# One step of a hybrid decoder on one core: rows before conditioning weights, output weights and samples first, one operation for the final norm

## The chip, the core and the metric

The kernel runs on one core of a Trainium2 chip. The metric is the device time of one execution in microseconds (us). TensorE (PE) multiplies, VectorE (DVE), ScalarE (ACT) and GpSimd (POOL) do the elementwise work, and the queue of SyncE (SP) issues nearly all loads and most stores. Every engine and every queue works through its own instructions in a fixed order that was laid down when the program was built.

## The reference, cut to what matters

One layer for a prompt of 2048 tokens and for 8 samples of 8 new tokens each (64 sample rows), all 1024 wide, in float32.

```python
ada = silu(c) @ w_ada + b_ada                  # conditioning: c is 1 + 8 rows, ada 6 x 1024 wide
sh_m, sc_m, g_m, sh_f, sc_f, g_f = split(ada, 6)
h = rmsnorm(x, norm_mix) * (1 + sc_m) + sh_m
rq, rk, rv, rg, sq, sk, sv = split(h @ w_in)
mix = concat(retention(rq, rk, rv) * silu(rg), stick_breaking(sq, sk, sv))
x = x + g_m * (mix @ w_out)
h = rmsnorm(x, norm_ffn) * (1 + sc_f) + sh_f
a = causal_conv3(h @ w_up_gate)
x = x + g_f * ((silu(a) * (h @ w_up_val)) @ w_down)
y = x * rsqrt(mean(x * x) + eps) * norm_final
```

The stick-breaking attention of the samples also reads 2048 cached positions per sample through a page table.

## The kernel before, in words

**Blocks and products.** The prompt is cut into four blocks of 512 tokens, each of four row tiles of 128 (`TILES`); the 64 sample rows ride with the first block in the projections and with the last block after attention. A float32 product is made of three products of a high and a low part (`mm3`, L310 to L312), or, for the 64 sample rows with their two parts side by side, of two (`tok_mm`, L319 and L320). A weight comes in as a 1 MB tile `raw` and is split into two tiles `whl`: ACT casts the high part (L183), DVE subtracts for the low part (L165).

**Who sets the order.** The functions are generators. `_weave` steps through several of them in proportion to the costs that they yield, and so fixes the order in which instructions are written down. A planner then runs through the instructions with a cost model of its own: on each engine and queue it takes, of those that are ready by its reckoning, the one written down first. So the order in the trace can differ from the order in the text, and on the chip each engine waits wherever the planned order puts something late in front.

**The head** (from L1490). The loads are written down in this order: conditioning rows `c9` and constants; the 2 MB of conditioning weights of column group 2 (a column group is 512 of the 6144 columns); the rows `hx` of the first block and of the samples (2.25 MB); column group 0; five small vectors into `vrows`; group 3 (into the two buffers of `wraw`); group 1. `ada` multiplies the conditioning rows by such a group (L531), copies the sums with ACT (L536), folds the partial sums by small products (L561) and writes coefficients with DVE (L568 or L572). It uses one buffer `ar`, into which the bias of each group is loaded in turn. `raw_features` norms each row tile (squares on ACT L399, root on POOL L392 and L165, scaling on DVE L590) and turns it on PE (L594, eight products a tile), with copies to `xT` (L598) that ACT and DVE share. `modulate` applies the coefficients of four of the eight feature groups k and splits the result into `act` (L605 to L612). Groups 2 and 0 serve k = 0 to 3, groups 3 and 1 serve k = 4 to 7. The first weights of the projection (`first_in`) are loaded and split after that, and `dense_pair` multiplies them: 96 products of 288 columns, 48 with k = 0 to 3 and 48 with k = 4 to 7. The caches' pages, the other conditioning groups and all four projection blocks follow, woven together, up to about 1240 us.

**The output block** (`out_block`). For the last block (`samp`) it loads, in this order, the gates of both halves (`load_g`), for each k the mixed features `act` and the samples' `smp` (eight loads of 64 KB), the rows `x` of the five tiles, and inside `w_tm` the output weights, two `raw` tiles for each half of 512 columns. Each k runs over the four row tiles and the samples; in the last two k of a half `by_tile` sorts by tile, the samples last. `residual` adds the result to `x`, `squares` and `rows_rstd` make the norm's root, and the generator `features` turns and modulates each tile for the next stage, the samples as the last of five. `ffn_block` of the block before drives it: one step before its last products (`next(feats, None)`), one after each of its four tiles, the rest after.

**The end** (`finish` inside `ffn_block`). The second half of each tile is squared by ACT (L1412), multiplied by the final weights `nf` by POOL (by DVE for the very last tile and in the other blocks), and, once POOL has made the root (`rows_rstd`), scaled by DVE with a one-tensor operation (L1417), beside ACT, which scales the first half (L1416). Then the tile is stored.

```python
            def finish(i, o, n, nf, eng):
                y = T(fp, [P, 2 * t], F32, "ff")
                act.activation(y[:n, :512], x2[i][:n, 512:], AF.Square, accum_out=ss[i][:n, 1:2])
                tt(eng, y[:n, 512:D], x2[i][:n, 512:], nf[:n], ALU.mult)
                yield
                r = rows_rstd(ss[i], n)
```

## Time and profile before

| what | us |
|---|---|
| median of 3 runs | 3336.03 (3325.15 to 3340.34) |
| the profiled execution, its own time | 3337.49 |
| its span, first to last instruction | 3335.8 |
| PE busy / DVE / ACT / POOL | 3201.6 / 2086.6 / 1580.0 / 1023.7 |
| mean granted TensorE clock | 0.98 of full |

A busy share says who works, not who is waited for; PE is busy for 96% of the span, so time can be won only where PE stands still, where it runs at the lower clock, or after its last product. The span is cut into stretches, and in each the instructions are read in order of time with the wait ahead of them. A row of such a list is: start, duration, engine, line, operation, result<-inputs, shapes and count, and in brackets the idle time of that engine just before and who ended it. Rows whose engine ends in q are a queue's issue of a transfer, not the transfer.

### The profile page before, as it was taken

The page shows a single profiled execution, that of the slowest core. Times are in us where ns is not written, and L with a number is a line of the kernel's source. Part 1 is how long each engine was busy: PE and PEld are TensorE (multiplying, and loading weights), DVE is VectorE, ACT ScalarE, POOL GpSimd, SP SyncE. Part 2 cuts the span into 40 slices and gives each one's busy share as a digit, 9 for nine tenths or more (in the row PEclk, how much of TensorE's full clock was granted, in tenths as well). Part 3 has the DMA queues.
Part 4 walks back from the last instruction along what each step waited for, and adds up shares of the span by engine and source line. Part 5 has one row for each costly group of instructions (what it writes and reads, how often), then busy time and mean ns, then how long its engine had stood idle before and what let it go on. Part 6 is the DMA issues. An engine that isn't in the chain of part 4 may idle for free. (4 is left out here: it accounts for less than half of the span.)

```text
span 3335.8 us, 50095 instructions
## 1 busy us (share of the span) xinstructions
PE 3201.6 (96%) x17879; PEld 2601.1 (78%) x17879; DVE 2086.6 (63%) x2989; ACT 1580.0 (47%) x2796; POOL 1023.7 (31%) x1841
## 2 busy tenths in 40 slices
PE   7999999999999889999999999999999999999998
PEld 5886777666887778878877778877788787799997
DVE  3245344245766587777778787787887873644445
ACT  3345335234444365555556455556555543533323
POOL 2012012013432343433444334344442432312113
PEclk8999999999999999999999999999999999999999
DMA  7757877885667843343454334354433335232221
GB/s 251 248 177 228 275 260 250 275 277 177 189 189 226 252 127 115 113 133 108 133 186 133 105 117 119 107 169 137 129 111 107 118 98 177 93 101 71 95 77 68
DMA packets 404247, 526.99 MB, mean 158 GB/s; under 512 B 25974, under 2 KB 242153, under 8 KB 403998
## 3 DMA queue, kind: packets, MB, share of 16 engines
q1 hardware_dynamic: 370078, 472.27, 45.3%
q10 hardware_dynamic: 33920, 51.52, 4.2%
q8 instruction: 142, 2.33, 0.3%
q14 instruction: 107, 0.88, 0.1%
HBM read 442.11 MB, written 81.60 MB: 157 GB/s over the span
## 5 line engine op out<-in xcount | busy, mean ns | idle before, releaser
L183 ACT CAST whl<-raw 128x1024 fp32r<-128x1024 f32 x408 | 427.5, 1049 | 1091.3 <-PE d L311 798.4
L165 DVE TENSOR_TENSOR whl<-raw,whl 128x1024 fp32r<-128x1024 f32 x408 | 517.8, 1270 | 577.0 <-ACT whl L183 568.8
L310 PE MATMUL d<-act,whl 128*128 128x512 f32 (+2 forms) x2016 | 745.0, 370 | 4.3 <-ACT whl L183 2.3
L312 PE MATMUL d<-act,whl 128*128 128x512 f32 (+2 forms) x2016 | 735.9, 365 | 1.2 <-DVE whl L165 1.2
L311 PE MATMUL d<-act,whl 128*128 128x512 f32 (+2 forms) x2016 | 733.7, 364 | 3.3 <-DVE act L165 2.4
L310 PEld LDWEIGHTS d<-act,whl 128*128 128x128 f32 x2016 | 384.8, 191 | 73.4 <-issue 11.1
L312 PEld LDWEIGHTS d<-act,whl 128*128 128x128 f32 x2016 | 383.9, 190 | 61.1 <-DVE whl L165 2.2
L311 PEld LDWEIGHTS d<-act,whl 128*128 128x128 f32 x2016 | 385.7, 191 | 58.7 <-DVE act L165 2.6
L310 PE MATMUL d<-whl,ff 128*128 128x512 f32 x704 | 279.3, 397 | 0.0
L311 PE MATMUL d<-whl,ff 128*128 128x512 f32 x704 | 278.8, 396 | 0.0
L312 PE MATMUL d<-whl,ff 128*128 128x512 f32 x704 | 278.1, 395 | 0.0
L310 PE MATMUL d<-whl,act 128*128 128x512 f32 x640 | 260.8, 409 | 10.3 <-ACT whl L183 9.2
L312 PE MATMUL d<-whl,act 128*128 128x512 f32 x640 | 258.5, 404 | 0.0
L311 PE MATMUL d<-whl,act 128*128 128x512 f32 x640 | 258.3, 404 | 0.0
L1172 DVE TENSOR_TENSOR_SCAN aom<-aom,acy 128x512 f32<-128x512 f32 x192 | 256.0, 1333 | 2.4 <-ACT aom L1158 1.7
L165 DVE TENSOR_TENSOR abe<-abe,aom 128x512 f32<-128x512 f32 (+2 forms) x320 | 229.7, 718 | 23.8 <-POOL abe L1162 2.3
L1196 PE MATMUL acc<-ahl,avv 128*128 128x512 f32 (+3 forms) x640 | 223.6, 410 | 15.2 <-DVE ahl L165 9.4
L1158 ACT ACTIVATE aom<-z,nb 128x512 f32<-128x512 f32 (+2 forms) x320 | 201.1, 628 | 61.2 <-PE z L1155 38.3
L1159 ACT ACTIVATE abe<-z,bb 128x512 f32<-128x512 f32 (+2 forms) x320 | 199.8, 624 | 0.0
L165 DVE TENSOR_TENSOR ahl<-z,ahl 128x512 fp32r<-128x512 f32 (+1 forms) x320 | 191.5, 598 | 10.7 <-ACT ahl L183 10.5
L1155 PE MATMUL z<-akk,aq 128*128 128x512 f32 (+3 forms) x640 | 190.5, 375 | 6.0 <-DVE ahl L165 3.1
L165 POOL TENSOR_TENSOR ff<-ff,hf 128x512 f32<-128x512 f32 (+1 forms) x101 | 161.0, 1624 | 90.2 <-DVE hf L165 76.2
(288 smaller groups left out, 5691.2 us busy)
## 6 DMA issues: line engine op xcount, KB each, us to landing
raw<-in_w_in SPq DMA_DIRECT2D x56, 1024.0 KB
raw<-in_w_up_gate SPq DMA_DIRECT2D x44, 1024.0 KB
raw<-in_w_up_val SPq DMA_DIRECT2D x44, 1024.0 KB
akk<-k SPq DMA_DIRECT2D x160, 256.0 KB
page<-in_cache_k_pages SPq DMA_DIRECT2D x128, 256.0 KB
vpage<-in_cache_v_pages SPq DMA_DIRECT2D x128, 256.0 KB
raw<-in_w_down SPq DMA_DIRECT2D x32, 1024.0 KB
raw<-in_w_ada SPq DMA_DIRECT2D x24, 1024.0 KB
```

The source lines that it names most:

```text
L165: eng.tensor_tensor(o, a, b, op)
L183: act.copy(hi, src)
L310: pe.matmul(ps, sh, mh, start=start, stop=False)
L311: pe.matmul(ps, sh, ml, start=False, stop=False)
L312: pe.matmul(ps, sl, mh, start=False, stop=stop)
L1155: pe.matmul(z[:, :n], qs[g, h][:, i * P : (i + 1) * P], kk[:, c, :n], start=c == 0, stop=c == 1)
L1158: act.activation(om[:, :n], z[:, :n], AF.Sigmoid, bias=nb[:, h : h + 1], scale=-SCALE)
L1159: act.activation(be[:, :n], z[:, :n], AF.Sigmoid, bias=bb[:, h : h + 1], scale=SCALE)
L1172: dve.tensor_tensor_scan(rv, rv, rv, init, ALU.mult, ALU.bypass)
L1196: pe.matmul(accs[0][:, cs], kv[u][1][:, kt, :], m[:, cs], start=(s == g and kt == 0 and c == 0), stop=(s == 0 and kt == NT - 1 and c == 1),)
```

## The change

The head: the four bias rows (into three `ar` buffers and one of the next pool) and the five vectors are loaded before the rows, the rows before any conditioning weights; groups 2 and 0 follow, then the first projection weights, then groups 3 and 1; the turns are written down ahead of all conditioning products, and the first half is modulated and the first weights are split ahead of groups 3 and 1. The output block of the last part: one load for all `smp`, the rows and gates written down after the second tile of output weights, the samples first in every loop, their features one step earlier. The end: `finish` loses its multiplication by `nf`, and the scaling after the root takes both factors in one operation (`scalar_tensor_tensor`), on DVE for all tiles.

```diff
@@ -209,7 +209,7 @@
...
     ]
-    mixs_sc = [T(dram, [P, 2, NS], F32, f"ms{k}") for k in range(KT)]
+    mixs_sc = T(dram, [KT, P, 2, NS], F32, "ms")
     gp_sc = [T(dram, [P, D], F32, f"gp{i}") for i in range(2)]
...
@@ -284,9 +284,13 @@
...
 
-    def w_fm(src, c0):
+    def raw_fm(src, c0):
         raw = next_raw().rearrange("p (a b) -> p a b", a=8)
         ld(raw, src[:, c0 : c0 + 256].rearrange("(k p) c -> p k c", p=P))
+        return raw
+
+    def w_fm(src, c0, raw=None):
+        raw = raw_fm(src, c0) if raw is None else raw
         for m in range(2):
...
@@ -361,7 +365,7 @@
...
         order = [(k, tile) for k in range(k0, k0 + 2) for tile in tiles]
-        return sorted(order, key=lambda kt: kt[1]) if k0 == n - 2 else order
+        return sorted(order, key=lambda kt: tiles.index(kt[1])) if k0 == n - 2 else order
 
...
@@ -491,7 +495,7 @@
...
     def vectors(pl):
-        rows = T(pl, [108, P], F32, "vrows")
+        rows = T(pl, [P, 512], F32, "hf")[:108, :P]
         for nme, o, n in (
...
@@ -518,15 +522,21 @@
...
 
+    def bias_row(pl, j):
+        ar = T(pl, [P, 512], F32, "ar")
+        ld(ar[P - 1 :, :], I["b_ada"][:, j * 512 : (j + 1) * 512])
+        return ar
+
     def ada(pl, s32, js, first=None):
...
         for j in js:
-            ar = T(pl, [P, 512], F32, "ar")
-            ld(ar[P - 1 :, :], I["b_ada"][:, j * 512 : (j + 1) * 512])
-            if first is not None:
+            if first is None:
+                ar = bias_row(pl, j)
+            else:
                 ps = pd()
-                for k0, raw in first.pop(j):
+                raws, ar = first.pop(j)
+                for k0, raw in raws:
                     for q in range(4):
...
@@ -534,7 +544,7 @@
...
                 act.copy(ar[: P - 1, :], ps[: P - 1, :])
-            else:
+            if first is None:
                 for k0, raw in w_rows(I["w_ada"][0], 0, KT, j * 512):
...
@@ -1252,12 +1262,13 @@
...
         xpool = xpools()
-        gates = [load_g(0, half, fp, samp and xpool) for half in range(2)]
+        ordered = tiles[NT:] + tiles[:NT]
         smp = T(xpool, [P, KT, 2, NS], F32R, "smp") if samp else None
+        gates = [] if samp else [load_g(0, half, fp, None) for half in range(2)]
         for k in range(KT):
             ld(acts[k // 4][:, k % 4, :, :TB], mix_sc[g][k])
-            if samp:
-                ld(smp[:, k], mixs_sc[k])
+        if samp:
+            ld(smp, mixs_sc.rearrange("k p c n -> p k c n"))
         x2, ss = [], []
...
@@ -1267,43 +1278,53 @@
...
 
-        for i, o, n in tiles:
-            x = T(xpool, [P, 1024], F32, "ff")
-            ld(x[:n], xp[g * TB + o : g * TB + o + n, :] if i < NT else xs)
-            x2.append(x)
-            ss.append(T(small, [P, 2], F32, f"os{i}"))
+        def rows():
+            if samp:
+                gates.append(load_g(0, 0, fp, xpool))
+            for i, o, n in tiles:
+                x = T(xpool, [P, 1024], F32, "ff")
+                ld(x[:n], xp[g * TB + o : g * TB + o + n, :] if i < NT else xs)
+                x2.append(x)
+                ss.append(T(small, [P, 2], F32, f"os{i}"))
+            if samp:
+                gates.append(load_g(0, 1, fp, xpool))
+
+        if not samp:
+            rows()
         for half in range(2):
...
             for k0, (hi, lo) in w_tm(w_out, 0, KT, half * 512):
-                for k, tile in by_tile(tiles, k0, KT):
+                if samp and half == 0 and k0 == 4:
+                    rows()
+                for k, tile in by_tile(ordered, k0, KT):
                     tok_mm(
...
                 tick()
-            for i, o, n in tiles:
+            for i, o, n in ordered:
                 residual(pss[i], gates[half][i == NT], x2[i], half, n, fp, dve if half else pool)
...
         tick(9)
-        rs = []
-        for i, o, n in tiles:
+        rs = {}
+        for i, o, n in ordered:
             squares(i, 1)
-            rs.append(rows_rstd(ss[i], n))
+            rs[i] = rows_rstd(ss[i], n)
 
...
                 if j >= 2:
-                    i, o, n = tiles[j - 2]
+                    i, o, n = ordered[j - 2]
                     to_features(xn[j - 2], o, n, coef[2], coef[3], acts, fp)
                 if j < len(tiles):
-                    i, o, n = tiles[j]
+                    i, o, n = ordered[j]
                     xa, xb = xn[j] = T(fp, [P, 512], F32, "c"), T(fp, [P, 512], F32, "a")
...
                     dve.tensor_scalar(xb[:n], x2[i][:n, 512:], rs[i][:n, 0:1], None, ALU.mult)
-                if j >= 1:
+                if j >= (2 if samp else 1):
                     yield 1.0
...
@@ -1407,14 +1428,13 @@
...
 
-            def finish(i, o, n, nf, eng):
+            def finish(i, o, n, nf):
                 y = T(fp, [P, 2 * t], F32, "ff")
                 act.activation(y[:n, :512], x2[i][:n, 512:], AF.Square, accum_out=ss[i][:n, 1:2])
-                tt(eng, y[:n, 512:D], x2[i][:n, 512:], nf[:n], ALU.mult)
                 yield
...
                 act.activation(y[:n, :512], x2[i][:n, :512], AF.Copy, scale=r[:n, 0:1])
-                dve.tensor_scalar(y[:n, 512:D], y[:n, 512:D], r[:n, 0:1], None, ALU.mult)
+                dve.scalar_tensor_tensor(y[:n, 512:D], x2[i][:n, 512:], r[:n, 0:1], nf[:n], ALU.mult, ALU.mult)
                 sv(O["y_prompt"][g * TB + o : g * TB + o + n, :] if i < NT else O["y_sample"], y[:n, :D])
...
@@ -1439,7 +1459,7 @@
...
                         residual(pss[tile[0]], gfs[half][tile[0] == NT], x2[tile[0]], half, tile[2], fp, dve)
-                        ends.append(finish(*tile, nf, pool if samp and tile[0] != NT - 1 else dve))
+                        ends.append(finish(*tile, nf))
                         next(ends[-1])
...
@@ -1490,28 +1510,24 @@
...
         with tile_pool("head", 2) as hp0:
-            hp = _Bufs(hp0, dict(hx=5, hj=1, xT=1, vrows=1, raw=4, ar=1))
-            rows_of = lambda j, pl=hp: list(w_rows(I["w_ada"][0], 0, KT, j * 512, pl))
-            xrows = first_rows(hp)
-            first = {2: rows_of(2)}
-            rows = list(xrows)
-            first[0] = rows_of(0)
+            hp = _Bufs(hp0, dict(hx=5, hj=1, xT=1, raw=4, ar=3))
+            rows_of = lambda j: list(w_rows(I["w_ada"][0], 0, KT, j * 512, hp))
+            bias = {j: bias_row(ip if j == 1 else hp, j) for j in (2, 0, 3, 1)}
             s32 = prep(hp, ip)
+            vectors(ip)
+            rows = list(first_rows(hp))
+            first = {j: (rows_of(j), bias[j]) for j in (2, 0)}
+            sq_raw = raw_fm(w_in, SQ)
             xT = T(hp, [P, KT, TB + NS], F32, "xT")
-            vectors(hp)
-            first[3] = rows_of(3, wraw)
-            feats = raw_features(hp, xT, rows)
-            for _ in ada(hp, s32, (2,), first):
+            for _ in raw_features(hp, xT, rows):
                 pass
-            for _ in feats:
+            for _ in ada(hp, s32, (2, 0), first):
                 pass
-            first[1] = rows_of(1)
-            for _ in ada(hp, s32, (0, 3), first):
+            first.update({j: (rows_of(j), bias[j]) for j in (3, 1)})
+            modulate(xT, coef[0], coef[1], acts, range(4))
+            first_in[0, 0, SQ] = list(w_fm(w_in, SQ, sq_raw))
+            for _ in ada(hp, s32, (3, 1), first):
                 pass
-            modulate(xT, coef[0], coef[1], acts, range(4))
-            for _ in ada(hp, s32, (1,), first):
-                pass
-            first_in[0, 0, SQ] = list(w_fm(w_in, SQ))
             modulate(xT, coef[0], coef[1], acts, range(4, 8))
...
```

## Rows read from the trace of the kernel before

**Rows 1.** Windows in the head: PE, PEld, DVE, ACT, POOL busy, clock, DMA share, GB/s.

```profile
20.00:30.00 10.00, 7.70 (x29) 1.13 (x21) 1.48 (x3) 0.00 (x0) 1.05 (x2) 1.00 1.05 382
...
50.00:60.00 10.00, 9.03 (x50) 8.64 (x49) 2.04 (x4) 3.94 (x6) 5.47 (x8) 0.50 0.20 72
...
90.00:100.00 10.00, 10.00 (x78) 9.98 (x77) 2.67 (x5) 2.88 (x7) 0.00 (x0) 1.00 1.03 322
```

**Rows 2.** PE in the head, in order of time.

```profile
27.79 1.92 PE L531 MATMUL d<-raw,s 128*32 128x512 f32 x2 [0.77 <-DMA raw<-in_w_ada]
...
31.37 6.94 PE L594 MATMUL z<-con,hx 128*128 128x128 f32 x36
...
46.46 0.61 PE L310 MATMUL d<-act,whl 128*128 128x288 f32 x1 [2.29 <-ACT whl L183]
...
71.00 0.29 PE L312 MATMUL z<-act,whl 128*128 128x288 f32 x1
```

**Rows 3.** DVE in the head: first rows scaled, and coefficients of both halves.

```profile
15.02 0.75 DVE L590 TENSOR_SCALAR hx<-hx,rs_b 128x1024 f32<-128x1024 f32 x1 [6.98 <-POOL rs_b L165]
...
41.71 0.20 DVE L568 COPY coef<-z 128x36 f32<-128x36 f32 x1 [2.94 <-PE z L561]
...
53.85 0.19 DVE L568 COPY coef<-z 128x36 f32<-128x36 f32 x1 [4.18 <-PE z L561]
```

**Rows 4.** SP's queue in the head.

```profile
2.96 1.96 SPq L171 DMA_DIRECT2D hx<-in_x_prompt  x4
...
9.95 2.21 SPq L171 DMA_DIRECT2D vrows<-in_norm_mix  x1
```

**Rows 5.** The last output block: DVE's split of the last down weights, SP's queue, the chain.

```profile
2804.77 1.23 DVE L165 TENSOR_TENSOR whl<-raw,whl 128x1024 fp32r<-128x1024 f32 x1 [3.76 <-ACT whl L183]
...
2814.96 1.50 SPq L171 DMA_DIRECT2D raw<-in_w_out  x2
...
2814.96 12.16 DMA raw<-in_w_out
```

**Rows 6.** PE in the last output block, and the window after its wait.

```profile
2828.30 1.22 PE L310 MATMUL d<-whl,act 128*128 128x512 f32 x2 [5.75 <-ACT whl L183]
...
2830.00:2840.00 10.00, 10.00 (x39) 7.93 (x39) 3.65 (x4) 1.99 (x2) 0.00 (x0) 0.86 0.30 107
```

**Rows 7.** Windows at the features of the last block, and its two releasing rows.

```profile
2880.00:2890.00 10.00, 6.61 (x38) 4.76 (x36) 7.45 (x14) 9.49 (x23) 3.93 (x3) 0.87 0.00 1
2890.00:2900.00 10.00, 7.30 (x36) 6.89 (x37) 8.99 (x26) 4.57 (x9) 3.04 (x4) 0.62 0.35 107
...
2889.94 0.68 DVE L165 TENSOR_TENSOR act<-hf,act 128x512 fp32r<-128x512 f32 x1
...
2893.54 0.61 PE z L311
```

**Rows 8.** The end: PE's last product, the last tile's steps, POOL on the chain.

```profile
3320.45 0.40 PE L312 MATMUL d<-whl,ff 128*128 128x512 f32 x1
...
3324.92 0.68 DVE L165 TENSOR_TENSOR hf<-d,gp 128x512 f32<-128x512 f32 x1
...
3327.40 0.68 DVE L165 TENSOR_TENSOR ff<-ff,hf 128x512 f32<-128x512 f32 x1
...
3329.43 0.61 ACT L1412 ACTIVATE ff<-ff 128x512 f32<-128x512 f32 x1
...
3317.09 2.94 POOL ff L165 x2
```

**Rows 9.** DVE with one tensor and with two: the end, and the convolution's line (min/median/max ns).

```profile
3328.80 0.49 DVE L1417 TENSOR_SCALAR ff<-ff,rs_b 128x512 f32<-128x512 f32 x1 [0.72 <-POOL rs_b L165]
...
L1354 DVE SCALAR_TENSOR_TENSOR c<-a,vecs,c x8: 734/743/777, 2048.3 to 2088.1; 128x512 f32<-128x512 f32 x8
```

**Rows 10.** Windows of the woven stretch, the whole and its worst 100 us.

```profile
140.00:1240.00 1100.00, 1037.01 (x6787) 810.87 (x6786) 568.24 (x1027) 478.37 (x892) 271.21 (x513) 0.97 0.70 225
1140.00:1240.00 100.00, 88.13 (x441) 71.44 (x440) 71.47 (x97) 58.13 (x114) 38.53 (x76) 0.93 0.55 156
```

## The prediction

> **What bounds the kernel now.** I read the windows first, then PE's list in order of time, then the queue and the engines that end its waits. In the woven stretch of 1100 us PE is busy for 1037 [rows 10]; there the products themselves are the bound, and nothing in this change touches them. So the change can only act where PE waits, where its clock is low, or after its last product, and it touches three such places.
>
> *The head.* The transfers run at 382 GB/s, as fast as anywhere here [rows 1], yet PE's order is what costs: the first rows are scaled by 15.77 us [rows 3], but their turns start at 31.37, behind conditioning products that wait for their weights until 27.79 [rows 2]. The coefficients of k = 0 to 3 follow at 41.71, those of k = 4 to 7 only at 53.85 [rows 3]; the first projection product starts at 46.46 and the last of the first pair ends at 71.29 [rows 2], much of it at half clock [rows 1]. *The last output block.* PE waits 5.75 us for output weights [rows 6] whose load was issued at 2814.96 and took 12.16 us [rows 5], and the clock is low after it. A second hole lies in the features, 2884 to 2897 [rows 7]. *The end.* After PE's last product (3320.85) the last tile's first DVE step starts at 3324.92 [rows 8], and the span ends at 3335.8.
>
> **The head, part by part.** The bytes are the same, their order is not. Up to the rows, SP now issues three loads as before and nine small ones. The nearest issue rows give 0.5 us each (four in 1.96) as the high side [rows 4]: the rows then start about 4.5 us after the three, at 2.96 - 1 + 4.5 = 6.5 at the latest, against 2.96 now. From 6.5 us, 382 GB/s carries 2.25 MB of rows and 4 MB of weights (groups 2 and 0) by 6.5 + 16.4 = 22.9, one more MB of first projection weights by 25.5, and groups 3 and 1 by 36.0. All of them were loaded before too, only the last MB has changed its place.
>
> From there: 1.92 us for the products of the last tile [rows 2] and, an estimate, 2 for copy, fold and coefficients: first coefficients at 26.8 instead of 41.71, second ones at 39.9 instead of 53.85. From coefficients to the first product it took 46.46 - 41.71 = 4.75 us. If the turns are done by then, PE starts the first 48 products at 31.6. If the planned order again puts the products of groups 2 and 0 ahead of the turns, as it does now, the turns (6.94 us and a rest, say 8.6) run from 24.8 to 33.4 and the first product comes at about 35.5. The products take 0.128 us each at full clock (78 in 10 us) and twice that at the low one [rows 1], so 48 cost 6.1 or 12.3. The second 48 cannot start before 39.9 + 4.75 = 44.7. The pair ends between 44.7 + 6.1 = 50.8 and 35.5 + 12.3 + 12.3 = 60.1, against 71.29: **a gain between 11.2 and 20.5**. I take **15**, a little under the middle, since the order on PE now is the unkind one. It reaches the end only if the woven stretch behind it is bound by PE, as rows 10 say (94% busy). Costed at nothing: bias rows in four buffers, vectors in another pool's tile, the first weights' split (ACT and DVE, beside the wait for groups 3 and 1); their cover is that transfer of 10.5 us, and without it the two splits would cost some 2 us each.
>
> What is moved past what: everything on SP behind the rows (groups 2 and 0) comes 2.25 MB or 5.9 us later than today. That is paid only if PE needs it earlier than 22.9, and today it uses group 0's products not before 41.71. Groups 3 and 1 wait for buffers that the products of 2 and 0 release, so a late turn delays them: free until about 25.5, one for one after that.
>
> **A rule against this.** The row says that a small load holds the queue for 2.21 us at worst, behind large loads in flight [rows 4]; placed in front of them it should cost its issue alone. The Trainium skill (DMA: Bandwidth & Descriptors, Anatomy of one DMA) gives each transfer on the GpSimd path a fixed cost of about 2 us, mostly completion, and calls small transfers descriptor-dominated (Bandwidth); if that were time on the queue, nine would cost 18 us by the page. The sum goes by the rows; the other reading is the second rival below.
>
> **The last output block.** The second tile of output weights needs a buffer that DVE frees at 2804.77 + 1.23 = 2806.00 [rows 5], 9 us ahead of today's issue. Ahead of it on SP now are gates, eight small loads instead of one, and five rows; these (nine loads, first wanted after 112 products, over 25 us at 39 in 10 us [rows 6]) go behind. Then PE's wait of 5.75 goes, and with it the slow stretch: clock 0.86 over 10 us is 2.8 us at half, and 1.7 us before 2830 [rows 6], so 4.5 us at half, a loss of 2.2. Sum 7.9. If the planner finds the rows ready first and leaves them in front, seven fewer loads still save about 7 x 0.49 = 3 [rows 4], of which 2 at least should reach PE, so the ends are 2 and 7.9. I take **7**. Late next: nothing, as the third tile is wanted only after the second's products. The samples' load must now be whole before the first product; today eight pieces come in turn. Its cover is the last products of the block before; without it, it would cost its own transfer, 0.5 MB at 382 GB/s = 1.4 us.
>
> Features: PE lacks 3.39 and 2.70 us in the two windows, and the clock is 0.62 in the second [rows 7]. The last release is the samples' low part (2893.54); the fourth row tile's is there at 2889.94 + 0.68 = 2890.62. With the samples first, the tail is the row tile: 2.9 us less. But the samples' steps now go ahead of four tiles on ACT (9.49 of 10 busy), so from 0 to 6 (all of the 6.1). I take **3**.
>
> **The end.** Five multiplications by `nf` go, four of them POOL's; the scaling grows from 0.49 to 0.74 us [rows 9], beside ACT's own scaling. At least POOL's 2.94 us on the chain go, less 0.25: 2.7 [rows 8]. At most all that the last tile waits behind earlier tiles: 3324.92 - 3320.85 = 4.07, 3327.40 - 3325.60 = 1.80 and 3329.43 - 3328.08 = 1.35, together 7.2. I take **5.5**, nearer the high end, as POOL's multiplications were what held up the roots. In the other blocks DVE also loses one operation a tile; PE's products are the cover there, and without it this would be a further gain, so I set nothing.
>
> **Sum.** 15 + 7 + 3 + 5.5 = 30.5. The profiled execution took 3337.49, 1.5 above the median of the runs shown, so 3307 in its terms and 3305.5 in those of the median: **3306**.
>
> **Rivals.** A measurement of this kernel can tell about 0.5% from no change, 16.7 us, so faster means under 3319.3.
>
> *The planner keeps its order.* The change states an order of text; if the rows stay ahead of the output weights and the samples win nothing, the block gives 2 instead of 10: 3336 - 22.5 = 3314. For it: the turns stand far from their place in the text today. Chance 0.17.
>
> *Small loads hold the queue.* If nine hold it for 2.21 us each, 19.9 instead of 4.5, all later loads slip by 15.4 us and the head gains nothing: 3336 - 15.5 = 3320. The same result comes if the woven stretch waits for pages or weights anyway and swallows the head's gain; its DMA share of 0.70 [rows 10] speaks against that. Together 0.16.
>
> *Slower.* The planner lays out the woven stretch anew, with key pages, projection weights and conditioning weights on SP in another order. PE's idle time there is 1100 - 1037 = 63 us; at the rate of the worst 100 us (11.87) it would be 130.6, 67.6 more [rows 10]: 3336 - 30.5 + 67.6 = 3373. It decides the sign once the idle time grows by over 30.5, to 93.5. Against it: only the stretch's start moves, and its text is unchanged. Chance 0.06.
>
> **Numbers.** The forecast has 0.61, the rivals 0.17, 0.16 and 0.06. Faster: 0.61 + 0.17 = 0.78; same 0.16; slower 0.06. The low ends give 11.2 + 2 + 0 + 2.7 = 15.9 (3320), the high ones 20.5 + 7.9 + 6 + 7.2 = 41.6 (3294.4). The runs shown lie 15.2 us apart, so a median of a few may be off by some 4 on either side: the range is 3290 to 3324. It takes in the first two rivals and leaves out the last.
>
> **What would show it.** Right: turns on PE ahead of 25 us, the first pair done by about 56, coefficients of k = 4 to 7 near 40; no wait at the second tile of output weights and no half clock after it; no POOL multiplication after 3317 and an end some 10 us after PE's last product instead of 15. Wrong: turns still behind conditioning products and the pair's end near 70; rows still ahead of output weights on SP; or all three places as said, and a later stretch that is longer by what the head has won.

## The result, and the profile of the changed kernel

The median of seven executions fell from 3336.03 us (3325.15 to 3345.58) to 3317.45 us (3312.19 to 3319.33). The ratio is 0.9943, with a 95% interval from 0.9932 to 0.9954: 18.6 us, or 0.56%. The interval is clear of 1, so the kernel is faster, by a little over the half per cent from which the prediction calls a change faster. The forecast of 3306 us was 11.5 too low; the range of 3290 to 3324 holds the result.

The profiled execution of the changed kernel took 3316.52 us (0.9 under its median) with a span of 3314.8 us, where the one before had 3335.8. Line numbers below are those of the kernel they are shown from: L310 to L312 of before, the three products of every dense step, are L314 to L316 in the changed one.

**The head.** The windows of the head (columns as in [rows 1]):

```profile
30.00:40.00 10.00, 5.93 (x28) 2.38 (x32) 6.04 (x6) 5.50 (x9) 4.22 (x5) 0.56 1.06 375
40.00:50.00 10.00, 10.00 (x64) 7.23 (x57) 1.41 (x5) 1.98 (x4) 2.35 (x8) 0.76 0.28 62
50.00:60.00 10.00, 10.00 (x81) 9.64 (x79) 4.68 (x6) 3.92 (x9) 4.93 (x11) 1.00 1.00 336
60.00:70.00 10.00, 7.74 (x52) 5.82 (x52) 4.47 (x7) 4.09 (x6) 0.00 (x0) 1.00 1.06 368
```

And TensorE there in order of time, beside [rows 2] (start, us, engine, line, operation, [idle before it, and what ended it]):

```profile
12.30 5.43 PE L604 MATMUL z<-con,hx 128*128 128x128 f32 x24 [4.14 <-DVE hx L600]
...
32.59 1.93 PE L541 MATMUL d<-raw,s 128*32 128x512 f32 x8 [3.67 <-DMA raw<-in_w_ada]
...
41.60 0.61 PE L314 MATMUL d<-act,whl 128*128 128x288 f32 x1
...
45.48 1.07 PE L541 MATMUL d<-raw,s 128*32 128x512 f32 x8
...
47.38 0.96 PE L571 MATMUL z<-con,ar 128*128 128x9 f32 x8
...
49.28 0.40 PE L314 MATMUL z<-act,whl 128*128 128x288 f32 x1
...
59.77 0.29 PE L316 MATMUL z<-act,whl 128*128 128x288 f32 x1
...
63.62 0.40 PE L314 MATMUL d<-act,whl 128*128 128x288 f32 x1 [2.26 <-ACT whl L183]
```

The turns (L604) now start at 12.30 instead of 31.37, as the change says. But the first projection product comes at 41.60, behind conditioning products of groups 3 and 1 (32.59 on, for whose weights TensorE first waits 3.67 us); the last of those stand among the projection products (45.48), and the fold that gives the second half of the coefficients is at 47.38. The pair's last product ends at 60.06 (before: 71.29). Then there is a wait that was not there before: 2.26 us at 63.62, for the next pair's weights. VectorE shows the two halves of the coefficients, beside [rows 3]:

```profile
28.96 0.20 DVE L578 COPY coef<-z 128x36 f32<-128x36 f32 x1 [3.44 <-PE z L571]
...
48.38 0.20 DVE L578 COPY coef<-z 128x36 f32<-128x36 f32 x1 [6.07 <-PE z L571]
```

SP's queue, beside [rows 4]: nine small loads (four biases, five vectors, of which the last is shown) go out in 3.3 us ahead of the rows, which start at 5.29.

```profile
1.94 1.16 SPq L171 DMA_DIRECT2D ar<-in_b_ada  x4
...
4.95 0.29 SPq L171 DMA_DIRECT2D hf<-in_sb_gn  x1
5.29 1.77 SPq L171 DMA_DIRECT2D hx<-in_x_prompt  x4
...
37.66 0.93 SPq L171 DMA_DIRECT2D rot<-in_rot  x2
48.41 0.25 SPq L171 DMA_DIRECT2D ar<-in_b_ada  x1
```

Between its last two rows SP is blocked for 9.8 us: group 4's bias wants the one row buffer that group 1's bias still holds, and the transfers idle (62 GB/s in 40 to 50 us).

**The last output block**, SP's queue, beside [rows 5]: the second weights tile goes out at 2791.27, the rows behind it at 2796.58. TensorE shows no wait in the block, and its windows (beside [rows 6]) are full, at full clock:

```profile
2790.63 0.59 SPq L171 DMA_DIRECT2D smp<-ms  x1
2791.27 3.83 SPq L171 DMA_DIRECT2D raw<-in_w_out  x1
...
2796.58 2.37 SPq L171 DMA_DIRECT2D ff<-in_x_prompt  x4
```

```profile
2800.00:2810.00 10.00, 9.98 (x44) 7.76 (x43) 2.68 (x2) 3.49 (x8) 5.66 (x5) 1.00 1.04 327
...
2860.00:2870.00 10.00, 7.01 (x40) 5.47 (x38) 9.96 (x16) 9.03 (x20) 2.96 (x2) 1.00 0.00 1
2870.00:2880.00 10.00, 5.86 (x30) 5.52 (x31) 9.20 (x13) 6.29 (x14) 4.95 (x8) 0.66 0.33 105
```

The last two rows are the features, beside [rows 7]. The hole is as large as before, with VectorE at 9.96 and ScalarE at 9.03 of 10 in its first half.

**The end**, VectorE in order of time, beside [rows 8]; TensorE's last product ends at 3301.69:

```profile
3304.17 0.75 DVE L1437 SCALAR_TENSOR_TENSOR ff<-ff,rs_b,gp 128x512 f32<-128x512 f32 x1 [1.20 <-POOL rs_b L165]
...
3305.44 0.68 DVE L165 TENSOR_TENSOR hf<-d,gp 128x512 f32<-128x512 f32 x1
...
3310.40 0.75 DVE L1437 SCALAR_TENSOR_TENSOR ff<-ff,rs_b,gp 128x512 f32<-128x512 f32 x1 [1.80 <-POOL rs_b L165]
```

POOL's multiplications are gone, and the last tile's first step (3305.44) is still 3.75 us behind its last product (before: 4.07). It waits behind the scaling of the tile before it, which waits for a root.

### The profile page after: what moved, and what is told of

The parts are those of the page before. It is cut to its first block, busy times and chain, and to the rows that moved or that the text cites. A ratio compares the mean times of both kernels' runs of the same rounds, so it can differ in the third digit from the quotient of the medians.

```text
span 3314.8 us, 50068 instructions
## 1 busy us (share of the span) xinstructions
PE 3184.6 (96%) x17879; PEld 2586.2 (78%) x17879; DVE 2087.0 (63%) x2976; ACT 1580.8 (48%) x2796; POOL 1016.2 (31%) x1837
## 5 line engine op out<-in xcount | busy, mean ns | idle before, releaser
L314 PE MATMUL d<-act,whl 128*128 128x512 f32 (+2 forms) x2016 | 743.1, 369 | 4.2 <-ACT whl L183 2.3
L316 PE MATMUL d<-act,whl 128*128 128x512 f32 (+2 forms) x2016 | 733.6, 364 | 0.0
L314 PEld LDWEIGHTS d<-act,whl 128*128 128x128 f32 x2016 | 382.9, 190 | 74.7 <-issue 12.8
L316 PEld LDWEIGHTS d<-act,whl 128*128 128x128 f32 x2016 | 382.2, 190 | 60.5 <-issue 1.2
L314 PE MATMUL d<-whl,ff 128*128 128x512 f32 x704 | 279.6, 397 | 0.0
L316 PE MATMUL d<-whl,ff 128*128 128x512 f32 x704 | 278.2, 395 | 0.0
L314 PE MATMUL d<-whl,act 128*128 128x512 f32 x640 | 259.9, 407 | 3.3 <-ACT whl L183 2.1
L316 PE MATMUL d<-whl,act 128*128 128x512 f32 x640 | 256.8, 401 | 0.0
L1375 DVE SCALAR_TENSOR_TENSOR c<-a,vecs,c 128x512 f32<-128x512 f32 x176 | 135.3, 769 | 81.0 <-ACT c L1372 46.1
```

The costliest lines, as they stand in the source:

```text
L314: pe.matmul(ps, sh, mh, start=start, stop=False)
L316: pe.matmul(ps, sl, mh, start=False, stop=stop)
L1375: dve.scalar_tensor_tensor(c[:, :TB], a[:, j : j + TB], cw(j), c[:, :TB], ALU.mult, ALU.add)
```

## How the runs are read

Each of the runs below but the last is one execution beside one of the kernel before (3344.93 us on the chip of e1 to e4, 3329.77 for e5, e6, e9 and e10, 3335.0 for e7, e8 and e11). Such whole times are too coarse for effects of 2 us. So they are read by stage: TensorE issues the same 11,520 dense products in every kernel, and the start of the k-th product in the kernel before, minus that in another, is what has been gained up to there. The columns: gained at k = 384 (about 108 us, the head); length of the woven stretch from k = 384 to 4000; gained over the output block (k = 8600 to 8700) and over the features (8800 to 9000); from the start of the last product to the span's end.

| kernel | time | head | stretch | block | features | end |
|---|---|---|---|---|---|---|
| before | 3337.49 | 0 | 1254.9 | 0 | 0 | 15.36 |
| changed | 3316.52 | 8.72 | 1254.1 | 7.55 | 0.51 | 13.51 |
| e1 | 3333.49 | 7.93 | 1255.1 | -0.86 | -0.28 | 15.31 |
| e2 | 3330.49 | 2.76 | 1257.4 | 7.03 | -0.27 | 15.23 |
| e3 | 3327.57 | 0.66 | 1248.0 | -0.46 | -0.48 | 13.56 |
| e4 | 3324.66 | 7.83 | 1262.2 | 7.67 | -0.41 | 13.51 |
| e5 | 3312.05 | 8.70 | 1251.7 | 7.65 | 0.49 | 11.50 |
| e6 | 3315.63 | 7.92 | 1252.5 | 7.39 | 0.91 | 13.55 |
| e7 | 3326.94 | 8.37 | 1264.9 | 7.79 | -0.54 | 13.59 |
| e8 | 3319.12 | 9.38 | 1250.7 | 1.26 | 0.22 | 13.56 |
| e9 | 3313.93 | 8.36 | 1251.8 | 7.70 | -0.40 | 13.46 |
| e10 | 3318.71 | 2.83 | 1250.8 | 6.99 | -0.29 | 13.51 |
| e11 | 3311.77 | 7.83 | 1249.0 | 7.44 | -0.39 | 13.53 |
| e12 | 3307.21 | 12.12 | 1250.8 | 7.57 | 0.75 | 11.51 |

The woven stretch, whose text none of these kernels changes, took from 1248.0 to 1264.9 us, although TensorE, VectorE, ScalarE and POOL do the same operations on the same tiles in the same order there in all fourteen executions. From k = 9000 to the last product all fourteen took 409.26 to 409.30. So much of what separates whole times lies in the stretch, and a number of the other columns is good to some 0.5 us (the head to 1 or 2: e2, whose head is that of before, has 2.76 there).

## The experiments

**e1, e2, e3: one place of the change each, in the kernel before.** e1 has the changes to the head and to `ada`, `vectors` and `w_fm` alone; e2 those of `out_block`, `by_tile` and the samples' scratch tensor; e3 those of `finish` and its caller.

> Only the head of the change. If the three places add up independently: the k-th dense product of TensorE runs 11 us earlier than before at the end of the first pair, 8.5 to 9 us right after it (a wait of 2.3 us for the next weights), 9 to 11 us earlier through the woven stretch and still there at 2790 us, and 8 to 11 us at the end; the wait of SP for the one row buffer of the adaLN bias (about 10 us, ended by the fold of group 1) is there too. Rival, the woven stretch swallows it: under 4 us left at 1240 us. Rival, the head's gain hangs on the later parts: another gain than 8 to 11 at 2780 us.

> Only the last block's output weights, samples and features. If independent: no shift (under 0.5 us) up to 2780 us, then 7 to 8 us gained over the output block (the TensorE wait of 5.75 us and the low clock behind it gone), 0 to 1 us more or less over the features, and 7 to 8.5 us in all, the tail as before (14.9 us from the last product to the end). Rival, the block's gain came from the head's shift of the attention it is woven with: under 4 us.

> Only the final norm. Theory, the tail is held by the planned alternation of the tiles on VectorE and ScalarE: the time from TensorE's last product to the end falls from 14.95 to 13 to 13.3 us (under 2 us gained), with VectorE and ScalarE waiting for rs_b between the tiles as in the changed kernel. Rival, POOL's multiplications were the hold, as predicted, and the other parts gave some of it back: 9 to 10 us are left. Nothing else moves by more than 0.5 us.

The three add up in their own places. e1 gains 7.93 in the head (8.72 in the changed kernel), e2 7.03 in the block (7.55), e3 1.80 at the end (1.85), each less than 1 us elsewhere, but for e2's head. So each part gains in its place without the others. In e3 VectorE waits for the same roots as in the changed kernel (1.20, 1.00 and 1.79 us before three of its scalings): the rival, by which 9 to 10 us would be left at the end, falls. What e1 expected behind the head did not hold: 9 to 11 us were to stay, and 7.77 were left at k = 4000 and 5.1 at k = 8600. By that number its second rival (another gain than 8 to 11 at 2780 us) is met. But from k = 4000 to 8600, where e1 loses 2.7 us against the kernel before, the other kernels stand anywhere from 0.2 lost to 3.4 gained, so one execution can't settle it.

Does the stretch swallow the head's gain? Over the ten kernels that are 7.8 to 12.1 us ahead at its start its mean length is 1254.3 us, over the four that are 0 to 2.8 ahead it is 1252.8. The gain is carried, within the scatter. The medians say the same: they differ by 18.6 us, by the interval 15 to 23, and the other three columns hold only 9.9 of it.

**e4: the wait of SP taken away.**

```diff
-    def bias_row(pl, j):
-        ar = T(pl, [P, 512], F32, "ar")
+    def bias_row(pl, j, tag="ar"):
+        ar = T(pl, [P, 512], F32, tag)
...
-            bias = {j: bias_row(ip if j == 1 else hp, j) for j in (2, 0, 3, 1)}
+            bias = {j: bias_row(*((ip, j, "kf") if j == 1 else (hp, j))) for j in (2, 0, 3, 1)}
```

> The changed kernel with group 1's bias row in another buffer, so that group 4's bias finds the row buffer free. Theory: SP no longer waits some 10 us there, the loads behind it (page table, weights of group 4, the next input weights) go out by 42 us, TensorE's wait of 2.26 us for the second pair's weights goes, and the gain of 11.2 us at the first pair's end is kept behind it: 2 to 3 us over the changed kernel at product 400 and at 1240 us. Rival, the second pair's weights are held by something else (a buffer of raw weights, the splits on ScalarE and VectorE): the wait of SP goes and the one of TensorE stays, no gain. Rival, the woven stretch levels it: the gain is there at 70 us and gone by 1240 us.

The wait of SP went and TensorE's stayed: my theory of it was wrong, the rival right. SP in e4, then TensorE, then ScalarE:

```profile
38.30 0.32 SPq L171 DMA_DIRECT2D ar<-in_b_ada  x1
...
43.12 0.42 SPq L171 DMA_DIRECT2D raw<-in_w_in  x1
```

```profile
62.97 0.40 PE L314 MATMUL d<-act,whl 128*128 128x288 f32 x1 [2.26 <-ACT whl L183]
```

```profile
61.26 0.22 ACT L656 COPY kf<-z 128x64 f32<-128x64 f32 x1
...
61.87 2.94 ACT L183 CAST whl<-raw 128x1024 fp32r<-128x1024 f32 x3 [0.40 <-ACT kf L656]
```

The weights were issued 6.67 us earlier (43.12, not 49.79), and the wait is the same 2.26 us: ScalarE does their split at 61.87 in its own order, behind the copies out of the first pair's banks.

**e5: the end's order written out.** The scalings of the prompt's tiles are put behind the last residual on VectorE and behind the last square on ScalarE.

```diff
+                with ExitStack() as held:
+                    for ins in lasts if after is None and i != NT else ():
+                        held.enter_context(tc.issue_after(ins.ins))
+                    act.activation(y[:n, :512], x2[i][:n, :512], AF.Copy, scale=r[:n, 0:1])
...
                         ends.append(finish(*tile, nf))
-                        next(ends[-1])
-                        if len(ends) > 1:
+                        lasts = next(ends[-1]), added
+                        if len(ends) > 1 and after is not None:
                             next(ends[-2], None)
-                    next(ends[-1], None)
+                    for end in ends:
+                        next(end, None)
```

> The changed kernel with the last block's order written out: VectorE does the residuals of all tiles and ScalarE their squares before either scales a tile of the prompt by its root (the samples' tile is scaled as before). Theory, the alternation of the tiles on VectorE and ScalarE holds the end: from TensorE's last product to the end 9.5 to 11 us where the changed kernel takes 13.5. Rival, the stores hold it: four of 512 KB go out close together and the time stays at 12.5 to 13.5 us. Rival, POOL's chain of root operations (about 1.1 us a tile) holds it: 11 to 12.5 us with ScalarE waiting for rs_b.

The end fell from 13.51 to 11.50 us. That is the band of the rival by which POOL's chain of roots holds (11 to 12.5, with ScalarE waiting for `rs_b`): the alternation was worth 2.0 us. What holds the end behind it is read from rows and was not tested. The last residual on VectorE, ScalarE's last square and scaling, and SP's stores at the end of e5:

```profile
3300.66 0.69 DVE L165 TENSOR_TENSOR ff<-ff,hf 128x512 f32<-128x512 f32 x1
```

```profile
3301.39 0.63 ACT L1433 ACTIVATE ff<-ff 128x512 f32<-128x512 f32 x1 [0.60 <-DVE ff L165]
...
3304.59 0.72 ACT L1438 ACTIVATE ff<-ff,rs_b 128x512 f32<-128x512 f32 x1 [0.64 <-POOL rs_b L165]
```

```profile
3302.75 2.99 SPq L171 DMA_DIRECT2D out_y_prompt<-ff  x4
```

The last residual (3301.35) ends 2.2 us after TensorE's last product, 5.2 in the changed kernel. The last scaling waits 0.64 us for its root, which comes 2.5 us after its square (3302.02), and from the last scaling's end (3305.3) to the span's end (3310.3) it is 5.0 us, against 3.7 in the changed kernel, where the stores were spread out.

**e6: the features in the old order.**

```diff
-                    i, o, n = ordered[j - 2]
+                    i, o, n = tiles[j - 2]
...
-                    i, o, n = ordered[j]
+                    i, o, n = tiles[j]
...
-                if j >= (2 if samp else 1):
+                if j >= 1:
```

> The changed kernel with the features of the last block in the old order (the samples' tile last, an interleaving step after the first tile). Theory, the order of the features is worth nothing, because ScalarE's and VectorE's work up to the last tile's features is the same and the wait only moved to another engine: TensorE's gain over before at product 9000 is 18.5 to 19.5 us as in the changed kernel. Rival, samples first did gain its 3 us and the earlier output block took them back: 15.5 to 17 us here.

Product 9000 stands 20.1 us ahead of before, 0.6 more than the band, for 0.91 us in this stage against 0.51 in the changed kernel (and -0.54 to 0.49 in the eight other kernels with samples first). Samples first is worth nothing, and rather less than the old order, which e12 has too (0.75). In e6 TensorE still waits 3.6 us for ScalarE's features, in the changed kernel 5.1; only the name of the late tile has changed.

**e7 and e8: the block's two edits one at a time.** e7 loads the samples in eight pieces again, e8 the gates and rows ahead of the second weights tile.

```diff
             ld(acts[k // 4][:, k % 4, :, :TB], mix_sc[g][k])
-        if samp:
-            ld(smp, mixs_sc.rearrange("k p c n -> p k c n"))
+            if samp:
+                ld(smp[:, k], mixs_sc[k])
```

```diff
-        if not samp:
-            rows()
+        rows()
...
-                if samp and half == 0 and k0 == 4:
-                    rows()
```

> The changed kernel with the last block's samples loaded in eight pieces between the loads of the prompt's features, as before; the output weights still go ahead of the rows. Theory, the place of the weights ahead of gates and rows is what took TensorE's wait of 5.75 us away: eight loads delay the second weights tile (2791.27 us in the changed kernel) by 0 to 6 us, which the first weights cover, and 6 to 7.6 us are still gained over the output block. Rival, the one load for the samples carried half of it: 2 to 5 us are gained.

> The changed kernel with gates and rows of the last block loaded ahead of the second weights tile again, the samples still in one load. Theory as for the run with eight loads: the weights come 5 to 9 us later than in the changed kernel and TensorE waits for them, so that 1 to 4.5 us are gained over the output block where the changed kernel gains 7.5. Rival, the one load carried it: 6 us or more are gained here too.

With both edits the block gains 7.55 us, without the one load 7.79, without the order 1.26. The order is the whole gain, as far as 0.5 us can be told. e8 issues the tile at 2798.48, behind the rows, and shows what the order had removed:

```profile
2797.92 0.47 PE L323 MATMUL z<-whl,smp 128*128 128x512 f32 x1 [1.43 <-DMA smp<-ms]
2811.25 0.50 PE L323 MATMUL z<-whl,smp 128*128 128x512 f32 x1 [2.36 <-ACT whl L183]
```

Its first row is what the one load can cost: the first product waits 1.43 us for all samples at once. The changed kernel shows no such wait.

**e9: the first pair's products ahead of groups 3 and 1.** The two halves of `dense_pair` become a generator, and the head runs its first half ahead of `ada(hp, s32, (3, 1), first)`.

```diff
-            first_in[0, 0, SQ] = list(w_fm(w_in, SQ, sq_raw))
+            first_in[0, 0, SQ] = dense_halves(list(w_fm(w_in, SQ, sq_raw)), acts, TB + NS, True)
+            next(first_in[0, 0, SQ])
```

> The changed kernel with the first pair's products of k = 0 to 3 put ahead of the products of groups 3 and 1 on TensorE. Theory, TensorE has work without a break from about 35 us in either order and what is left is its own time at the low clock: the first product starts at 35 to 37.5 us, the second half of the coefficients comes 2 to 6 us later than 48.4 us, and the last product of the first pair stands within 2 us of the changed kernel's. Rival, the planned order cost the head 4 to 7 us: the pair's end is 4 us or more earlier. Rival, it gets worse: the second half of the features is late and TensorE waits 3 us or more before k = 4.

The first product came 8.7 us earlier, at 32.85; the second half of the coefficients at 48.48 (48.38), the pair's last product at 60.32 (59.77). The first two are not what was expected, the third is: in the net the planned order cost the pair's end nothing. But the window of 50 to 60 us shows a price of e9's order, a granted clock of 0.66 (the mean of stretches at its two levels, 1.2 and 2.4 GHz) where the changed kernel has 1.00, so what the order is worth at the same clock stays open:

```profile
50.00:60.00 10.00, 9.83 (x56) 9.51 (x57) 4.49 (x7) 4.01 (x9) 5.00 (x11) 0.66 0.95 329
```

**e10: the next weights' split ahead of the evictions**, on top of e4.

```diff
             for _ in ada(hp, s32, (3, 1), first):
                 pass
+            begun = w_fm(w_in, SK)
+            next_in[SK] = chain([next(begun)], begun)
```

> The kernel with group 1's bias elsewhere, and besides the first split of the second pair's weights written ahead of the first pair's products, so that ScalarE does it before the evictions of that pair. Theory, formed on the run before: TensorE's wait of 2.26 us at 63 us comes from ScalarE's order (evictions ahead of a split whose weights had landed 10 us earlier), not from SP: the wait goes, with it the drop of the granted clock to 0.83 in 60 to 70 us, and product 128 is 2 to 4 us earlier than in that run. Rival, the two free buffers of split weights are taken until the first pair ends: no change. Rival, the next split (the pair's second half) becomes late: the wait of 2 us moves to product 110 or 128 and the gain is under 1 us.

It lost 5.9 us in the head against the changed kernel, in a way that no theory had, though TensorE's wait behind the pair went, as expected. Moving the split in the text changed TensorE's planned order as well. In the changed kernel 24 products of k = 0 to 3, those of the second half of the columns, fill the time from 49.28 us on, up to the first operands of k = 4. In e10 they stand at 57.03, behind products of k = 4 to 7, and TensorE waits 1.49 us for the cast of k = 4, which comes when it did (49.33, there 49.34). ScalarE, then TensorE:

```profile
49.33 0.67 ACT L622 CAST act<-xT 128x576 fp32r<-128x576 f32 x1
49.91 1.04 ACT L183 CAST whl<-raw 128x1024 fp32r<-128x1024 f32 x1
...
50.86 1.25 ACT L622 CAST act<-xT 128x576 fp32r<-128x576 f32 x2
```

```profile
50.05 0.53 PE L314 MATMUL d<-act,whl 128*128 128x288 f32 x2 [1.49 <-ACT act L622]
...
57.03 0.61 PE L314 MATMUL z<-act,whl 128*128 128x288 f32 x1
```

```profile
50.00:60.00 10.00, 8.98 (x41) 8.09 (x42) 4.04 (x4) 3.49 (x6) 5.57 (x11) 0.57 0.34 126
```

The split itself (1.04 us) stands behind that cast and ahead of the next ones. Of the three breaks of TensorE from 48 to 54 us, 2.5 us together, it can have lengthened only the last and shorter one (0.62 us, for a low part that POOL makes from such a cast). Behind the breaks the clock was low for much of the window, 0.57 on the mean.

**e11: groups 3 and 1 between the two weight tiles.**

```diff
+            parts = first_in[0, 0, SQ] = dense_halves(list(w_fm(w_in, SQ, sq_raw)), acts, TB + NS, True)
+            next(parts)
             for _ in ada(hp, s32, (3, 1), first):
                 pass
+            next(parts)
```

> The changed kernel with the products of groups 3 and 1 put between the two weight tiles of the first pair's k = 0 to 3. Theory, formed on the two runs before: what the head still loses is low clock and the breaks of TensorE that bring it, because the second half of the coefficients came at 48.4 us in either order. Here they come at 41 to 45 us, TensorE starts products at 32 to 34 us and has no break above 1 us up to the pair's end, the granted clock of 50 to 60 us stays at 1.00, and product 64 stands 3 to 7 us ahead of the changed kernel's 55.66 us; 1 to 6 us of it are left at product 128, where the second pair's weights are next to be late. Rival, the clock falls in 50 to 60 us all the same or the weights of the second pair take all of it back: product 128 within 1 us of the changed kernel's 69.14 us.

The clock held at 1.00 from 40 to 60 us and products began at 32.99, as expected. The rest fell: the coefficients came at 48.84, since the plan still put twelve products ahead of group 1's last ones, and the wait for the second pair's weights, now 2.91 us, took back what there was. Product 128 stands at 69.92, within 1 us of the changed kernel's: the rival.

**e12: together.** e11 with the second tile's products behind the last of group 1, the early split of e10 behind `modulate(..., range(4, 8))`, and e5 and e6.

```diff
+            with tc.issue_after(products[-1].ins):
+                next(parts)
...
             modulate(xT, coef[0], coef[1], acts, range(4, 8))
+            begun = w_fm(w_in, SK)
+            next_in[SK] = chain([next(begun)], begun)
```

> The changed kernel with what the runs suggest: all products of groups 3 and 1 between the two weight tiles of the first pair's k = 0 to 3 (the second tile's products put behind the last of them), the next weights' load and first split behind the second half of the features, the end's residuals ahead of its scalings, and the features of the last block in the old order. Theory: the end of the head hangs on the second half of the coefficients, which the plan put at 48.4 to 48.8 us in three orders though its weights had landed by 40 us; here they come at 42 to 45 us, product 64 at 47 to 51 us (55.66 in the changed kernel), product 128 at 61 to 66 us (69.14), TensorE's wait for the second pair's weights is under 1 us; with 2 us at the end and 0.5 us at the features 5 to 10 us under the changed kernel, so 24 to 30 us under the kernel before. Rival, TensorE's own time is the bound of the head: product 128 within 1.5 us of the changed kernel's, 2 to 4 us gained in all. Rival, a break of TensorE near 50 us lets the granted clock fall and product 128 is later than in the changed kernel.

Median of six 3305.16 us (3303.95 to 3317.24), against 3335.18 of ten before: ratio 0.9916, interval 0.9899 to 0.9933, 30.0 us. It beats both kernels, the changed one by 12.3 us of the medians, which were not taken side by side. By stage: 12.12 in the head, 7.57, 0.75 and 3.85 at the end, 24.3 together; the other 6 us of its profile lie in the stretch (4.1) and between it and the block (1.9). The order in its stretch is that of the other kernels on the four engines, with one weights load moved on SP; whether those 6 us are the kernel's or luck, one profile can't say.

The head's 3.4 us more did not come as expected. The coefficients came at 47.26, product 64 at 52.79, and the pair's last product started at 58.84, only 0.9 earlier than in the changed kernel. What changed is what follows: the second pair's weights are issued at 27.86 (49.79), their split stands at 50.67 in ScalarE's order, the second pair starts without a wait, and the clock stays up.

```profile
58.84 0.29 PE L316 MATMUL z<-act,whl 128*128 128x288 f32 x1
58.98 0.29 PE L314 MATMUL d<-act,whl 128*128 128x288 f32 x1
```

```profile
60.00:70.00 10.00, 10.00 (x75) 7.82 (x73) 1.23 (x5) 2.30 (x6) 0.00 (x0) 1.00 0.95 316
```

## Why the prediction was right, and where it was wrong

The sign and the three places were right. The four terms of the sum, 15 + 7 + 3 + 5.5 = 30.5, measured 8.7 + 7.55 + 0.5 + 1.85 = 18.6. That this is just what the medians differ by is partly luck: the two profiled executions differ by 21.0, of which 0.8 lie in the woven stretch and 1.6 between it and the output block. The forecast was 11.5 us off, a range of 34 us held the result, and 18.6 is close to the sum of the low ends, 15.9: two terms of the four lie under their own low ends. Of the signs that the prediction named, the turns came ahead of 25 us, the wait and the low clock at the second weights tile went, and so did POOL's multiplications; the first pair's end (60.06, not 56), the second coefficients (48.38, not 40) and the end (13.1 us after the last product, not 10) did not come as named.

**The head: 15, measured 8.7.** The step that put the pair's end between 50.8 and 60.1 took in the result only at its last end, 60.06. (The 8.7 are against one execution of the kernel before; e2 and e3 have its head too and are 2.8 and 0.7 ahead of it, and against the mean of the three the seven executions with the new head, e1 and e4 to e8 among them, gain 7.3.) Two things in the step failed. First, the places of the products: the first was to start at 31.6 to 35.5 and came at 41.60, and the second coefficients, on whose 39.9 the low end rests, at 48.38, although TensorE waits for no weights of group 1. In three other orders (e9, e11, e12) the coefficients came at 47.3 to 48.8, and the pair's last product started at 58.8 to 60.3, although products began at 33 us. What the sum had left out is TensorE's other work in the same stretch, here from e12:

```profile
39.91 1.92 PE L549 MATMUL d<-raw,s 128*32 128x512 f32 x16
42.52 1.06 PE L579 MATMUL z<-con,ar 128*128 128x9 f32 x8 [0.69 <-ACT ar L554]
43.52 1.92 PE L549 MATMUL d<-raw,s 128*32 128x512 f32 x14
...
46.26 0.95 PE L579 MATMUL z<-con,ar 128*128 128x9 f32 x8
...
53.28 0.85 PE L528 MATMUL z<-con,raw 16*128 16x16 f32 x11
...
56.12 0.85 PE L528 MATMUL z<-con,raw 16*128 16x16 f32 x11
```

Groups 3 and 1, their folds and the convolution state's turns: 7.6 us in these rows and 1.9 more at 34.58, beside 96 products of 0.13 us, 12.6: 22.1 of the 25.8 us from the first product to the end of the last. TensorE in e12 has no break above 0.7 us there: its own work is the bound, and in the four orders tried the pair's last product moves by 1.5 us. The rest is two breaks (0.69 and 0.61) and the low clock at its start (0.66 on the mean in 30 to 40 us), behind a break of 4.5 us ahead of the first product; an order without that break was not tried. Second, the sum said of no one who is late next behind the pair. It was the second pair's split on ScalarE: 2.26 us at 63.62, and the gain fell from 11.2 to between 8.6 and 9.1. e12, which has that split early, keeps 12.1. That the rows' rate and issue were right (rows on SP at 5.29, predicted 6.5 at the latest; first coefficients at 28.96, predicted 26.8) did not help.

**The rule weighed.** Nine small loads took SP 3.3 us, 0.27 to 0.29 each, so they did not hold the queue, and the reading of 18 us falls with its rival. The Trainium skill (DMA: Bandwidth & Descriptors, Anatomy of one DMA) puts most of the fixed cost of a transfer on the GpSimd path, about 2 us, into its completion. These nine went over SP's queue; issues of 0.27 to 0.29 us agree with it, and no row here shows a completion by itself.

**The output block: 7, measured 7.55.** The mechanism and the size were right, and e7 and e8 show that all of it is the weights' place. "Its cover is the last products of the block before": partly gone in e8, where the samples' load costs 1.43 us, and whole in the changed kernel.

**The features: 3, measured 0.5.** The step "the tail is the row tile: 2.9 us less" failed. It followed the last release of one tile, in a stretch in which ScalarE and VectorE are full (9.03 and 9.96 of 10); whichever tile is last, the same work stands ahead of it. The prediction had that as its low end, and should have taken it.

**The end: 5.5, measured 1.85**, under the low end of 2.7. The step that failed is "At least POOL's 2.94 us on the chain go", and with it the reason for taking more, that POOL's multiplications held up the roots. The row of 2.94 us ends at 3320.03, ahead of TensorE's last product (3320.85), so it could not come off the time behind that product in full. Behind the product the chain of the kernel before has one multiplication of POOL; and VectorE's scalings beside that one and beside the one before it took 1.48 and 1.49 us instead of 0.49, which the sum did not have either (the chain, then VectorE):

```profile
3325.97 1.23 POOL ff L165
```

```profile
3326.00 1.48 DVE L1417 TENSOR_SCALAR ff<-ff,rs_b 128x512 f32<-128x512 f32 x1 [0.40 <-POOL rs_b L165]
```

What stayed is the alternation: VectorE and ScalarE work the tiles in turn, and each scaling waits for a root behind which the next tile's residual and square stand. e3 shows the 1.8 us without any other part, e5 gets 2.0 more by order alone.

**The rivals.** The planner did obey at the output weights; that the samples win nothing, the other half of that rival, came true. The stretch did not swallow the head's gain, and it was not laid out anew: from k = 384 to 4000 the four engines and SP's queue have the same order as before, and it took 1254.1 us against 1254.9.

## What to carry to other kernels

Count what else an engine has to do in a stretch before pricing an earlier start: an operand that comes earlier (the first coefficients here by 12.75 us) is worth only what that engine's own work leaves, and the next operand behind it has to be early too. Where an in-order engine alternates between a step that waits and a step that others wait for, the order of the two can be worth as much as making either shorter (2.0 us here, against 1.8 for the multiplications); put the steps that feed others first. And where a planner sets the order, read every engine's order again after an edit: e10 moved one step on ScalarE, and the longest break that followed came from what TensorE's order had become. With the same split in another place and TensorE's order held by hand, e12 won 3.4 us.

## What the runs showed of the hardware

After the same break of 2.26 us before the second pair the granted clock of 60 to 70 us was 1.00 in the changed kernel and in e8, but 0.83 in e1, e4, e5, e6 and e7, and the next 32 products took 5.5 us in the first two and 7.0 to 7.1 in the others. So behind one and the same break the clock fell in five of seven executions, at a cost of 1.5 us.

POOL's small root step `rs_a` took 0.19 us alone and 0.58 us beside VectorE's scaling with two tensors, which ended 0.06 us before it (at 3300.56). A split on VectorE that took 1.23 us alone [rows 5] took 3.53 beside a run of POOL's additions in the output block, and ended 1.1 us after that run (2828.10). The rows are of the changed kernel, POOL's list and VectorE's:

```profile
3300.04 0.58 POOL L396 TENSOR_SCALAR rs_a<-sst 128x1 f32<-128x1 f32 x1
...
3303.31 0.19 POOL L396 TENSOR_SCALAR rs_a<-sst 128x1 f32<-128x1 f32 x1
```

```profile
2825.66 3.53 DVE L165 TENSOR_TENSOR whl<-raw,whl 128x1024 fp32r<-128x1024 f32 x1
```

The Trainium skill (SBUF — State Buffer, SBUF: two separate sides) has the two engines take a shared pair of ports in turn, each for a whole instruction; these rows agree with it in kind. And the 3616 products of the woven stretch took from 1248.0 to 1264.9 us in fourteen executions with the same order on four engines, while the last 2519 agreed to 0.04 us. Most of that spread is TensorE's busy time: 1198.1 us in the longest (e7), 1183.8 in the shortest (e3), at a mean granted clock of 0.97 and 0.98.
